# Layer B attention: scores three steps ahead instead of two from step 11 on, with a fourth buffer for the softmax weights

## The chip, the cores and the metric

The kernel runs on one core of one Trainium2 chip. Such a core has five engines that run side by side, each through its own list of instructions, in that list's order: TensorE (PE in the profile), which multiplies matrices and also transposes them; VectorE (DVE); ScalarE (ACT); GpSimd (POOL); and SyncE (SP), which here only starts transfers. An engine waits when its next instruction needs something that another engine has not yet delivered; nothing behind that instruction can overtake it.

TensorE writes its results to PSUM, and everything else (operands, weights, softmax weights) lies in SBUF. PSUM is used here as eight banks of 128 partitions by 512 numbers: the kernel takes six of them for matrix products (tag `mm`) and two for transposes (tag `tr`).

The metric is the device time of one execution in microseconds (us), the median over the runs of a kernel; lower is better.

## The reference

The program is a two-layer decoder trunk on 512 tokens of width 1024, all in 32-bit floating point. Layer A is a latent attention with eight heads over all earlier tokens, layer B is a sliding-window attention. After each comes an MLP with a squared ReLU. The part that matters here is the attention of layer B, for 16 query heads of 64 dimensions that share 4 key and value heads:

```python
s = einsum('bnqkgd,bnjkd->bnkgqj', q, k_band) * SWA_HEAD_DIM ** -0.5   # blocks of 128 queries, bands of 256 keys
s = where(mask, s + bias, -inf)          # relative-position bias, window of 128, causal
m = maximum(s.max(-1), sink)
p = exp(s - m[..., None])
denom = p.sum(-1) + exp(sink - m)
p = p / denom[..., None]
o = einsum('bnkgqj,bnjkd->bnqkgd', p, v_band)
y = o.reshape(B, S, 1024) @ w_o
x = layernorm(alpha * x + y)
```

## The kernel before

**Precision.** Each operand is kept as a rounded high part and a low part that holds the rest. A product is the sum of three products of parts (`three`), and a `split` is one ScalarE copy (the high part) and one subtraction on VectorE or GpSimd (the low part). In the score products of layer B the query holds both parts stacked along its 128 rows, so that two matmuls suffice.

**Order of the work.** The kernel is written as one list of calls. A scheduler at compile time fixes every engine's list from it: TensorE's instructions and most transfers are held in the order of the program (`pe(...)` says so), while those of VectorE, ScalarE and GpSimd are taken, when their engine is free in the scheduler's own clock, from those that are ready, those that stand earlier in the program first; what is traced under `high_priority` goes ahead of that. Buffers are given out in the same pass: a tile of a tag gets one of the tag's buffers once it is free, and its first writer waits for the last reader of the tile that was there.

**Layer B's attention** is run by `run_steps` (L552) with one step per head, `u = 0 ... 15`, after two steps that only start things (`ahead = 2`). Step `u` does, in TensorE's order:

1. `scores(u + 2)` (L1331): eight matmuls into two new `mm` banks, four query blocks in all. Then, off TensorE: VectorE adds the bias in place and takes the row maxima (L1354, four times) and makes from them the negative maxima `nb` (L1358); ScalarE takes the four exponentials from the two banks into the SBUF tile `p` with the row sums (L1362) and the sink's term `ri` (L1366); VectorE adds and inverts (L1367, L1368); GpSimd scales `p` by the result (L1369, L1371).
2. the fills that are due at this step: other work of TensorE that is put between the heads. Up to step 10 these are the queries of later heads (`queries`, 12 matmuls a call, two calls for a pair of heads); from step 11 on they are the first parts of the output projection, `proj.part(t, kp)` of L501, six matmuls each, which add the weight chunk `kp` to the projection of the token block `t`. The bank of a token block is taken at its first part and kept until the projection is finished.
3. `turn(u)` (L1374): seven transposes of `p` of head `u` into the two `tr` banks; ScalarE and VectorE split them to `pth` and `ptl` (L77, L81), which frees the `tr` banks.
4. `mix(u - 1)` (L1397): eight matmuls of values and transposed weights into one `mm` bank; ScalarE copies half of it (`low`, L1413), VectorE adds the other half (`o`, L1414), which frees the bank. After every second head ScalarE and GpSimd split `o` to `oh` and `ol` (L77, L81), the operands of the output projection.

The fills around the change are

```python
fill.append((0, 11, 11, preloads[1]))
for t, kp, u in ((0, 0, 11), (0, 1, 12), (1, 0, 13), (1, 1, 13), (2, 0, 14), (2, 1, 14), (0, 2, 15), (1, 2, 15), (2, 2, 16)):
```

that is, token block 0 takes its bank at step 11, block 1 at step 13, block 2 at step 14; `preloads[1]` starts two transfers of the following MLP's weights. The last two queries (heads 14 and 15) are made in one bank by `queries(7, 0)` and `queries(7, 1)`; this bank becomes free when VectorE has made the low part of head 15's query (L1326).

**Buffers.** `p` of layer B has three buffers of 4 KiB a partition, the transposed weights two each, the small tiles `nb`, `sm` and `ri` three each. The pool of layer B's attention lies in SBUF where the pool of the last MLP lies afterwards.

Of the kernel before, what the change touches and what calls it, by code (L numbers as in the profile page):

```python
# [8 lines left out]
F32 = mybir.dt.float32  # L9
# [6 lines left out]
P = 128  # L16
D = 1024
S = 512
NT = S // P
# [6 lines left out]
SQH, SKVH, SHD = 16, 4, 64  # L26
# [15 lines left out]
AHEAD_S, AHEAD_B = 3, 2  # L42
# [6 lines left out]
def build(tc, nc, io, out):  # L49
    with ExitStack() as top:  # L50
        cp = top.enter_context(tc.tile_pool(name="cp", bufs=1))
# [10 lines left out]
        def nm(s):  # L62
            n_names[0] += 1
            return f"{s}_{n_names[0]}"
# [10 lines left out]
        def split(dst_h, dst_l, src, engine=None, keep=False):  # L75

            high = nc.scalar.activation(dst_h, src, AF.Copy)  # L77
            if keep:
                pe(high)
            with behind(state.pop("open", None)):  # L80
                low = (engine or nc.vector).tensor_sub(dst_l, src, f32(dst_h))  # L81
            if pinned[0] and engine is None:
                pe(low)
            return high, low

        def pe(ins):
            tc.keep_in_program_order(ins)
# [15 lines left out]
        def group(dst, pairs, first=True, last=True, **kw):  # L103
            for i, (st, mv) in enumerate(pairs):
                pe(nc.tensor.matmul(  # L105
                    dst, st, mv, start=first and i == 0, stop=last and i == len(pairs) - 1, **kw
                ))
# [252 lines left out]
        nc.gpsimd.memset(f32(zeros), 0.0)  # L360
        b = bank()
        group(b.rearrange("p (a b) -> p a b", a=4), [(zeros, zeros[:, None, :].broadcast_to([P, 4, P]))] * WARM)
        dummy = cp.tile([P, 1], F32, name="dummy")

        x0 = Feat()
        xraw = [xp.tile([P, 4, S], F32, tag="xt", bufs=8, name=nm("xraw")) for _ in range(2)]
# [40 lines left out]

        ident = cp.tile([P, P], F32, name="ident")
        pe(nc.sync.dma_start(ident, io["ident"]))
        gq = cp.tile([P, 3], F32, name="gq")  # L410
        pe(nc.sync.dma_start(gq, io["g_q"]))
        gkv = cp.tile([P, 2], F32, name="gkv")
        pe(nc.sync.dma_start(gkv, io["g_kv"]))
        sink = cp.tile([P, SQH], F32, name="sink")
        pe(nc.sync.dma_start(sink, io["sinks"].partition_broadcast(P)))
# [3 lines left out]
        pe(small)  # L419
        relh, rell = [cp.tile([33, SQH], F32R, name=nm("rel")) for _ in range(2)]  # L420
        split(relh, rell, relb)
        half = cp.tile([P, 1], F32, name="half")
        nc.gpsimd.memset(half, -0.5)
        sink8 = cp.tile([P, SQH], F32, name="sink8")
        nc.vector.tensor_scalar(sink8, sink, 8.0, None, ALU.mult)
# [123 lines left out]
                    for t in range(NT):  # L549
                        self.evac(t, slice(512, D), bs[t])  # L550

        def run_steps(units, ahead, scores, turn, mix, fill, per, lag, rest):  # L552

            total = sum(f[0] for f in fill)
            n, spent, at = len(units), 0.0, 0
            for u in range(-ahead, n):
                if u + ahead < n:
                    scores(*units[u + ahead])  # L560
                target = total * (u + ahead + 1) / (n + ahead)
                while at < len(fill) and (spent < target or fill[at][1] <= u) and fill[at][2] <= u:
                    fill[at][3]()
                    spent += fill[at][0]
                    at += 1
                if u < 0:
                    continue
                turn(*units[u])
                if u >= lag and (u - lag) % per == per - 1:
                    mix(units[u - lag][0])  # L570
            for f in fill[at:]:
                f[3]()
            for f in rest:
                f()
            for u in range(n, n + lag):
                if (u - lag) % per == per - 1:
                    mix(units[u - lag][0])
# [339 lines left out]
        with tc.tile_pool(name="mla", bufs=1) as mp:  # L917
# [222 lines left out]
            def scores(h, i):  # L1140
                a = heads[h]
                kk = a["k"]
                qh, ql = a["q"]
                n = (i + 1) * P
                tq = slice(i * P, n)
                b = bank()
                p = scratch()
                mask = cmask[:, 512 - n :]
                if i == 0:

                    two = b[:, 0:256].rearrange("p (a b) -> p a b", a=2)
                    group(
                        two, [(qh[:, tq], kk[:, :, :n]), (a["qr"][:, tq], krr[:, :, :n])], True, False,
                        skip_group_check=True,
                    )
                    group(b[:, :n], [(ql[:, tq], kk[:, 0, :n])], False, True, skip_group_check=True)
                    nc.vector.tensor_add(p[:, :n], b[:, n : 2 * n], mask)
                    mask = p[:, :n]
                else:
                    group(  # L1160
                        b[:, :n],
                        three(qh[:, tq], ql[:, tq], kk[:, 0, :n], kk[:, 1, :n])
                        + [(a["qr"][:, tq], khh[:, :n]), (a["qr"][:, tq], kll[:, :n])],
                    )
                if i == 0:
                    for name in ("mx", "nb", "sm", "ri"):
                        a[name] = sp.tile([P, NT], F32, tag=name, bufs=3, name=nm(name))
                mx, nb, sm, ri = a["mx"], a["nb"], a["sm"], a["ri"]
                one = slice(i, i + 1)
                nc.vector.tensor_tensor_reduce(  # L1170
                    out=b[:, :n], in0=b[:, :n], in1=mask, op0=ALU.add, op1=ALU.max,
                    scale=1.0, scalar=NEG, accum_out=mx[:, one],
                )
                nc.vector.tensor_scalar(nb[:, one], mx[:, one], -MLA_SCALE, None, ALU.mult)
                nc.scalar.activation(
                    p[:, :n], b[:, :n], AF.Exp, bias=nb[:, one], scale=MLA_SCALE, accum_out=sm[:, one]
                )
                nc.vector.reciprocal(ri[:, one], sm[:, one])
                nc.vector.tensor_scalar(p[:, :n], p[:, :n], ri[:, one], None, ALU.mult)
                a["p", i] = p  # L1180
# [38 lines left out]
            fill = []  # L1219
# [34 lines left out]
        with tc.tile_pool(name="swa", bufs=1) as mp:  # L1254
# [76 lines left out]
            def scores(h, _):  # L1331
                j = h // GRP
                q = qs[h]
                nb = sp.tile([P, NT], F32, tag="nb", bufs=3, name=nm("nb"))
                sm = sp.tile([P, NT], F32, tag="sm", bufs=3, name=nm("sm"))
                ri = sp.tile([P, NT], F32, tag="ri", bufs=3, name=nm("ri"))
                bs = []
                for n2 in range(2):
                    b = bank().rearrange("p (a b) -> p a b", a=2)
                    bs.append(b)  # L1340
                    for a in range(2):
                        n = 2 * n2 + a
                        lo_c = P if n == 0 else 0
                        kc = slice(0, P) if n == 0 else slice((n - 1) * P, (n + 1) * P)
                        tq = slice(n * P, (n + 1) * P)
                        group(b[:, a, lo_c:], [(q[:, tq], khh[j][:, kc]), (q[:, tq], kll[j][:, kc])])

                mx = bs[0][:, 0, 0:NT]
                for n2 in range(2):
                    for a in range(2):  # L1350
                        n = 2 * n2 + a
                        lo_c = P if n == 0 else 0
                        b = bs[n2]
                        nc.vector.tensor_tensor_reduce(  # L1354
                            out=b[:, a, lo_c:], in0=b[:, a, lo_c:], in1=bias[h // 2][:, h % 2, lo_c:], op0=ALU.add,
                            op1=ALU.max, scale=1.0, scalar=NEG, accum_out=mx[:, n : n + 1],
                        )
                nc.vector.tensor_scalar(nb, mx, sink8[:, h : h + 1], -SWA_SCALE, ALU.max, ALU.mult)  # L1358
                p = mp.tile([P, NT, 256], F32, tag="p", bufs=3, name=nm("p"))
                for n in range(NT):  # L1360
                    lo_c = P if n == 0 else 0
                    state["exp"] = nc.scalar.activation(  # L1362
                        p[:, n, lo_c:], bs[n // 2][:, n % 2, lo_c:], AF.Exp, bias=nb[:, n : n + 1],
                        scale=SWA_SCALE, accum_out=sm[:, n : n + 1],
                    )
                nc.scalar.activation(ri, nb, AF.Exp, bias=sink[:, h : h + 1])  # L1366
                nc.vector.tensor_add(sm, sm, ri)  # L1367
                nc.vector.reciprocal(ri, sm)  # L1368
                nc.gpsimd.tensor_mul(p[:, 0, P:], p[:, 0, P:], ri[:, 0:1].broadcast_to([P, P]))  # L1369
                rest = ri[:, 1:].unsqueeze(2).broadcast_to([P, NT - 1, 256])  # L1370
                nc.gpsimd.tensor_mul(p[:, 1:, :], p[:, 1:, :], rest)  # L1371
                ps_of[h] = p
# [46 lines left out]
            fill = []  # L1419
# [13 lines left out]
            for m in range(2):  # L1433
                for part in range(2):
                    queries(m, part)
            run_steps([(h, 0) for h in range(SQH)], AHEAD_B, scores, turn, mix, fill, 1, 1, [])

        gb = lambda: load_gb("mix", 1)
        with tc.tile_pool(name="mlp1", bufs=1) as mp:
# [114 lines left out]
```

## Time and profile before

| | us |
|---|---|
| median of three runs | 994.83 |
| lowest and highest of them | 994.56, 996.27 |
| the profiled execution | 995.48 |
| span of its instructions | 993.7 |
| outside the span | 1.78 |
| TensorE busy in the span | 983.7 |
| ScalarE, VectorE, GpSimd busy in the span | 554.3, 773.5, 220.8 |

The profiled execution is 0.65 us above the median and inside the spread of the runs. The profile gives each instruction a start and a duration. Matmuls overlap: one begins before the one before it has ended, so the space between two starts, not a row's own duration, is what one costs when they follow each other, and an idle time that the profile prints (from a modelled end to the next start) is somewhat shorter than the time that was lost. In the rows below, a time is in us from the start of the span, then comes the duration, engine, source line, operation and "written <- read" by the names of the tiles; `x2` marks two instructions shown as one row; a square bracket at the end gives the idle time before it and what ended it.

### The profile page before, as it was taken

Reading aid. Unit: us, or ns where it says so; the run is one execution under the profiler, and the core shown is the slowest. Engines: PE = TensorE matmul, PEld = TensorE weight load, DVE = VectorE, ACT = ScalarE, POOL = GpSimd, SP = SyncE. Lnnn points to the kernel's source line nnn. Section 1 sums busy time; section 2 is a strip of 40 time slices with the busy share of each in tenths; the row PEclk is TensorE's granted clock in tenths of the full one; section 3 lists DMA queues with packets and bytes.
Section 4 is the critical chain, followed back from the end, with each engine's and each line's share of the span. In section 5 each row is a group of like instructions: output and inputs, shape, how many; then the busy total and the mean of one; then the engine's idle time right before and its main releaser. Section 6 shows DMA issues by size and latency. Waiting matters only on the chain.

```text
span 993.7 us, 15822 instructions
## 1 busy us (share of the span) xinstructions
PE 983.7 (99%) x6103; PEld 887.6 (89%) x6103; DVE 773.5 (78%) x1240; ACT 554.3 (56%) x850; POOL 220.8 (22%) x205
## 2 busy tenths in 40 slices
PE   9999999999999999999999999999999999999997
PEld 9888888998899999998898998889998998999986
DVE  6589858989679779786686778798985986898756
ACT  5557643567447537646146799446763663664620
POOL 1331001121312212210002765412121122023000
PEclk9999999999999999999999999999999999999999
DMA  7421237389789878954132213349798698798422
GB/s 262 145 88 43 86 127 208 106 168 236 134 190 238 163 170 229 226 98 148 64 107 96 86 65 103 121 106 213 201 186 186 172 211 173 164 265 144 115 94 85
DMA packets 60678, 149.55 MB, mean 150 GB/s; under 512 B 5259, under 2 KB 10300, under 8 KB 60604
## 3 DMA queue, kind: packets, MB, share of 16 engines
q0 software_dynamic: 24320, 58.73, 33.0%
q1 hardware_dynamic: 36140, 89.56, 26.8%
q8 instruction: 48, 0.79, 0.3%
q10 hardware_dynamic: 144, 0.26, 0.1%
q14 instruction: 26, 0.21, 0.1%
HBM read 146.41 MB, written 4.22 MB: 152 GB/s over the span
## 4 chain that ended last, share of the span: by engine, by line
PE 91%; DVE 3%; DMA 3%; ACT 1%; issue 1%; POOL 0%; DVEq 0%; ACTq 0%; POOLq 0%
PE mm L105 84%; PE tr L105 4%; DMA wq<-in_up 2%; PE tr L1191 1%; DVE wl L81 1%; PE tr L1382 1%; DVE x L456 1%; DVE x L459 1%; DMA raw<-in_w_v 1%; PE tr L1384 0%; ACT wh L77 0%; ACT p L1362 0%; PE tr L698 0%; POOL wl L81 0%; DVE bn L587 0%
## 5 line engine op out<-in xcount | busy, mean ns | idle before, releaser
L105 PE MATMUL mm<-wh,fac 128*128 128x512 f32 (+1 forms) x944 | 292.7, 386 | 0.0
L77 ACT ACTIVATE wh<-wq 128x1024 fp32r<-128x1024 f32 x164 | 173.6, 1060 | 183.8 <-PE mm L105 129.8
L81 DVE TENSOR_TENSOR wl<-wq,wh 128x1024 fp32r<-128x1024 f32 x164 | 199.6, 1221 | 70.6 <-ACT wh L77 69.8
L105 PE MATMUL mm<-xth,wh 128*128 128x256 f32 (+1 forms) x928 | 243.5, 290 | 0.3 <-DVE a L816 0.3
L105 PE MATMUL mm<-xth,wl 128*128 128x256 f32 (+1 forms) x800 | 233.2, 292 | 0.0
L105 PEld LDWEIGHTS mm<-wh,fac 128*128 128x128 f32 x944 | 176.2, 188 | 35.5 <-DVE fac L81 0.8
L105 PE MATMUL mm<-xtl,wh 128*128 128x256 f32 (+1 forms) x672 | 197.1, 293 | 0.0
L105 PE MATMUL mm<-wl,fac 128*128 128x512 f32 (+1 forms) x472 | 182.3, 386 | 0.0
L105 PEld LDWEIGHTS mm<-xth,wh 128*128 128x128 f32 x928 | 168.6, 192 | 3.6 <-issue 0.4
L105 PEld LDWEIGHTS mm<-xth,wl 128*128 128x128 f32 x800 | 153.2, 192 | 2.6
L77 ACT ACTIVATE wh<-raw 128x1024 fp32r<-128x1024 f32 (+3 forms) x86 | 84.9, 989 | 88.9 <-PE mm L105 55.9
L105 PEld LDWEIGHTS mm<-xtl,wh 128*128 128x128 f32 x672 | 128.7, 192 | 3.0
L203 POOL DMA_DIRECT2D wq<-in_up x64 | 77.5, 1237 | 200.7 <-DVE wl L81 193.5
L105 PEld LDWEIGHTS mm<-wl,fac 128*128 128x128 f32 x472 | 88.8, 188 | 16.6
L81 DVE TENSOR_TENSOR wl<-raw,wh 128x1024 fp32r<-128x1024 f32 (+2 forms) x64 | 74.8, 1176 | 32.3 <-ACT wh L77 32.0
L203 POOL DMA_DIRECT2D wq<-in_down x48 | 42.0, 875 | 189.1 <-DVE wl L81 183.2
L81 POOL TENSOR_TENSOR wl<-raw,wh 128x1024 fp32r<-128x1024 f32 (+2 forms) x22 | 46.8, 2130 | 91.4 <-ACT wh L77 69.0
L429 POOL TENSOR_TENSOR rs<-mv,half 128x1 f32<-128x1 f32 x16 | 8.8, 552 | 215.4 <-DVE mv L450 215.4
L105 PE MATMUL mm<-wh,oh 128*128 128x512 f32 x128 | 50.9, 398 | 0.7 <-ACT p L1362 0.7
L105 PE MATMUL mm<-wh,ol 128*128 128x512 f32 x128 | 50.1, 392 | 0.0
L105 PE MATMUL mm<-wl,oh 128*128 128x512 f32 x128 | 50.1, 391 | 0.1
L597 DVE TENSOR_TENSOR x<-mm,x 128x512 f32<-128x512 f32 (+1 forms) x49 | 32.9, 675 | 15.8 <-PE mm L105 15.7
(222 smaller groups left out, 1821.1 us busy)
## 6 DMA issues: line engine op xcount, KB each, us to landing
wq<-in_up POOLq DMA_DIRECT2D x64, 512.0 KB, 8.3
wq<-in_down POOLq DMA_DIRECT2D x48, 512.0 KB, 6.4
wq<-in_up SPq DMA_DIRECT2D x32, 512.0 KB, 5.9
raw<-in_down SPq DMA_DIRECT2D x28, 512.0 KB, 6.9
wq<-in_down SPq DMA_DIRECT2D x24, 512.0 KB, 5.5
raw<-in_up SPq DMA_DIRECT2D x16, 512.0 KB, 4.1
raw<-in_w_o SPq DMA_DIRECT2D x8, 512.0 KB, 4.6
raw<-in_w_sq SPq DMA_DIRECT2D x8, 512.0 KB, 3.2
```

Of the source, the lines that this page charges most:

```text
L77: high = nc.scalar.activation(dst_h, src, AF.Copy)
L81: low = (engine or nc.vector).tensor_sub(dst_l, src, f32(dst_h))
L105: pe(nc.tensor.matmul(dst, st, mv, start=first and i == 0, stop=last and i == len(pairs) - 1, **kw))
L203: nc.gpsimd.dma_start(half(a, jp), chunk(*more, jp), accum_op=ALU.add)
L429: state["rs"] = nc.gpsimd.tensor_tensor(r, v, half, ALU.pow)
L456: pin(nc.vector.scalar_tensor_tensor(x, x, mv[:, 0:1], gb[0], ALU.subtract, ALU.mult))
L459: state["norm"] = nc.vector.scalar_tensor_tensor(x[:, c], x[:, c], r, gb[1][:, c], ALU.mult, ALU.add)
L597: nc.vector.tensor_add(xs[t][:, c], b, xs[t][:, c])
L1191: pe(nc.tensor.transpose(pt[:, kb * P : (kb + 1) * P], p[:, kb * P : (kb + 1) * P], ident))
L1382: pe(nc.tensor.transpose(pt[:, a, 0:P], p[:, kb, P:256], ident))
```

## The change

Three things are changed.

- `run_steps` gets an argument `wider`. From step `wider` on, scores are issued up to three steps ahead instead of two. Layer B passes 11, layer A passes nothing. So at step 11 the scores of heads 13 and 14 are issued one after the other, ahead of that step's fills; at step 12 those of head 15; at step 13 none. Nothing moves before step 11, and no matmul is added or removed.
- `p` of layer B gets four buffers instead of three.
- Four small tiles of the permanent pool (`dummy`, `half`, `gq`, `gkv`) become slices of one tile `few`. Each took a slot of its own; together they give back 96 bytes a partition. The fourth buffer takes 4 KiB of SBUF a partition.

```diff
+        few = cp.tile([P, 8], F32, name="few")
+        dummy, half, gq, gkv = few[:, 0:1], few[:, 1:2], few[:, 2:5], few[:, 5:7]
-        dummy = cp.tile([P, 1], F32, name="dummy")
...
-        gq = cp.tile([P, 3], F32, name="gq")
-        gkv = cp.tile([P, 2], F32, name="gkv")
...
-        half = cp.tile([P, 1], F32, name="half")
...
-        def run_steps(units, ahead, scores, turn, mix, fill, per, lag, rest):
+        def run_steps(units, ahead, scores, turn, mix, fill, per, lag, rest, wider=None):
...
+            begun = 0
             for u in range(-ahead, n):
-                if u + ahead < n:
-                    scores(*units[u + ahead])
+                more = wider is not None and u >= wider
+                while begun < min(u + ahead + 1 + more, n):
+                    scores(*units[begun])
+                    begun += 1
...
-                p = mp.tile([P, NT, 256], F32, tag="p", bufs=3, name=nm("p"))
+                p = mp.tile([P, NT, 256], F32, tag="p", bufs=4, name=nm("p"))
...
-            run_steps([(h, 0) for h in range(SQH)], AHEAD_B, scores, turn, mix, fill, 1, 1, [])
+            run_steps([(h, 0) for h in range(SQH)], AHEAD_B, scores, turn, mix, fill, 1, 1, [], 11)
```

## The prediction

> **What bounds the kernel now.** First the page's busy times, then TensorE's waits in layer B, then the windows of the three steps concerned.
>
> ```profile
> span 993.7 us, 15822 instructions
> PE 983.7 (99%) x6103; PEld 887.6 (89%) x6103; DVE 773.5 (78%) x1240; ACT 554.3 (56%) x850; POOL 220.8 (22%) x205
> ...
> PE mm L105 <- ACT p L1362: 0.7, 1, 0.7
> PE tr L1382 <- DVE ptl L81: 0.3, 1, 0.3
> ...
> 604.80:609.39 4.59, 4.24 (x31) 3.62 (x31) 3.75 (x14) 4.05 (x11) 1.82 (x2) 1.00 0.17 68
> 609.39:613.47 4.08, 4.08 (x31) 3.77 (x31) 3.87 (x15) 3.79 (x13) 1.29 (x1) 1.00 0.02 6
> 613.47:618.20 4.73, 4.03 (x22) 3.25 (x22) 4.02 (x17) 4.65 (x16) 3.06 (x3) 1.00 0.00 0
> ```
>
> TensorE is busy for 99% of the span, and in layer B only two of its waits belong to the stretch that changes: one of 0.7 us for the exponentials (L1362), one of 0.3 us for the split of transposed weights. The window rows (length, then PE, PEld, DVE, ACT, POOL, then clock 1.00) show that around them VectorE and ScalarE are nearly full too: 3.87 of 4.08 us and 4.65 of 4.73 us. So the most that an earlier start of scores can win is about those two waits, and two full engines stand behind what it asks for.
>
> Now TensorE's own list through these steps (first rows of each piece; the row at 614.34 is the last score matmul).
>
> ```profile
> 604.80 0.27 PE L105 MATMUL mm<-skh,q 128*128 128x128 f32 x1
> ...
> 605.79 0.40 PE L105 MATMUL mm<-wh,oh 128*128 128x512 f32 x1
> ...
> 606.95 0.39 PE L105 MATMUL mm<-wh,ol 128*128 128x512 f32 x1
> 607.68 0.30 PE L1382 MATMUL tr<-ident,p 128*128 128x128 f32 x1 [0.35 <-DVE ptl L81]
> ...
> 608.42 0.36 PE L105 MATMUL mm<-pth,vv 128*128 128x256 f32 x1
> ...
> 609.39 0.27 PE L105 MATMUL mm<-skh,q 128*128 128x128 f32 x1
> ...
> 610.43 0.40 PE L105 MATMUL mm<-wh,oh 128*128 128x512 f32 x1
> ...
> 611.82 0.27 PE L1382 MATMUL tr<-ident,p 128*128 128x128 f32 x1
> ...
> 612.50 0.36 PE L105 MATMUL mm<-pth,vv 128*128 128x256 f32 x1
> ...
> 613.47 0.27 PE L105 MATMUL mm<-skh,q 128*128 128x128 f32 x1
> ...
> 614.34 0.28 PE L105 MATMUL mm<-skl,q 128*128 128x256 f32 x1
> 615.32 0.50 PE L105 MATMUL mm<-wh,oh 128*128 128x512 f32 x1 [0.70 <-ACT p L1362]
> ...
> 618.20 0.27 PE L1382 MATMUL tr<-ident,p 128*128 128x128 f32 x1
> ```
>
> Read in order: scores 13, projection part (0,0), turn 11, mix 10, scores 14, part (0,1), turn 12, mix 11, scores 15, parts (1,0) and (1,1), turn 13. Six projection matmuls start 1.16/5 = 0.23 apart (605.79 to 606.95), so part (0,0) is done feeding at 607.18 and turn 11 begins 0.50 late; the score matmuls end feeding at 614.34 + 0.12 = 614.46 and part (1,0) begins 0.86 late. From 605.79 to 618.20 are 12.41 us: 11.05 of work and 1.36 of waits.
>
> **The change part by part.** *Moved:* scores 14 from 609.39 to 605.79, scores 15 from behind mix 11 to behind mix 10. No matmul is added; scores cost 1.04 (609.39 to 610.43) and 0.99 us wherever they stand. What decides is the banks. At 605.79 I count the six `mm` banks as: heads 12 (two, its exponentials run), 13 (two, just written), the queries of 14 and 15 (one), mix 9 (one). Before, part (0,0) and mix 10 take head 12's two as the exponentials end; scores 14 come later and take those of the queries and mix 9. After, scores 14 take head 12's two, and part (0,0), next on TensorE, finds none free. When does one come free?
>
> ```profile
> 604.54 0.20 ACT L1362 ACTIVATION_READ_ACCUMULATOR p<-mm,nb 128x1 f32 x1
> ...
> 605.44 0.20 ACT L1362 ACTIVATION_READ_ACCUMULATOR p<-mm,nb 128x1 f32 x1
> ...
> 605.72 0.96 ACT L77 ACTIVATE pth<-tr 128x512 fp32r<-128x512 f32 x2
> 606.71 0.59 ACT L1325 ACTIVATE q<-mm 64x512 fp32r<-64x512 f32 x1
> ...
> 610.15 0.62 ACT L77 ACTIVATE oh<-o 128x512 fp32r<-128x512 f32 x1
> 610.80 0.37 ACT L1362 ACTIVATE p<-mm,nb 128x128 f32<-128x128 f32 x1
> ...
> 612.41 0.21 ACT L1362 ACTIVATION_READ_ACCUMULATOR p<-mm,nb 128x1 f32 x1
> 612.70 0.98 ACT L77 ACTIVATE pth<-tr 128x512 fp32r<-128x512 f32 x2
> ...
> 623.36 0.98 ACT L77 ACTIVATE pth<-tr 128x512 fp32r<-128x512 f32 x2 [2.14 <-PE tr L1384]
> ```
> ```profile
> 608.38 0.69 DVE L1326 TENSOR_TENSOR q<-mm,q 64x512 fp32r<-64x512 f32 x1
> 609.11 0.68 DVE L1414 TENSOR_TENSOR o<-mm,low 64x512 f32<-64x512 f32 x1
> 609.82 0.22 DVE L1358 TENSOR_SCALAR nb<-mm,sink 128x4 f32<-128x4 f32 x1
> 609.96 1.14 DVE L81 TENSOR_TENSOR ptl<-tr,pth 128x512 fp32r<-128x512 f32 x2
> ...
> 612.40 0.43 DVE L1354 CUSTOM_DVE_ANT_0 mm<-mm,bias 128x256 f32<-128x256 f32 x1
> ...
> 612.87 0.43 DVE L1354 CUSTOM_DVE_ANT_0 mm<-mm,bias 128x256 f32<-128x256 f32 x1
> ...
> 623.99 1.16 DVE L81 TENSOR_TENSOR ptl<-tr,pth 128x512 fp32r<-128x512 f32 x2 [1.04 <-ACT pth L77]
> ```
>
> Head 12's banks are free at 604.74 and 605.64, so scores 14 do not wait: 605.79 to 606.83. The queries' bank is free when VectorE ends head 15's low part, 608.38 + 0.69 = 609.07; mix 9's at 609.11 + 0.68 = 609.79. I keep VectorE's order up to there, since what scores 14 add stands behind it in the program. The hand-over from VectorE to TensorE I take from the chain of work that ended last, ahead of turn 11:
>
> ```profile
> 607.55 0.14 issue
> ```
>
> **First new stall:** 609.07 + 0.14 = 609.21, less 606.83 = **2.38 us**, before a part that waited for nothing. Bounds: 1.30, if VectorE took the query as soon as ScalarE has it (606.71 + 0.59 = 607.30, + 0.69 + 0.14 = 608.13); 3.1, if mix 9's bank is the one given. Behind the waiting matmul stand turn 11, mix 10 and scores 15, and ScalarE's split of turn 11.
>
> Then part (0,0) 1.39, turn 11 0.74, mix 10 0.97 (by the starts above): scores 15 at 612.31. Their banks are head 13's. ScalarE, with turn 11 not there, makes `oh` at 609.85, and 0.65 later (610.15 to 610.80) head 13's exponentials, 1.90 long (610.80 to 612.70): 610.50 to 612.40. The first bank is free a little before scores 15 want it, the second (612.32) half a microsecond later than the first: no wait. Scores 15 end at 613.30, part (0,1) at 614.69; turn 12 wants the `tr` banks of turn 11.
>
> **Second new stall.** Those are free after ScalarE's and VectorE's split of turn 11, which is ready at 611.3. But head 14's exponentials may now go ahead: VectorE, behind `nb` at 609.82, makes the four biases of head 14 at 0.47 each (612.40 to 612.87), 609.96 to 611.84, and its `nb` by 612.1, ahead of 612.40, when ScalarE comes free. They stand earlier in the program than turn 11, so I let them go first: 612.40 to 614.30. Then the split begins on ScalarE, VectorE follows 0.63 behind (623.36 to 623.99) for 1.16: second `tr` bank free at 616.09, and mix 11, in place of 614.69 + 0.68 = 615.37, starts 0.14 and three transposes (0.24) later, at 616.47: **1.10 us**. Bounds: 0, if the split goes first (VectorE is through at 614.2), and 1.9, the exponentials' length.
>
> **Stalls that go:** 0.50 and 0.86, and 0.1 for the slow restart at 615.32 (615.32 to 618.20 is 2.88 for twelve matmuls at 0.23). Turn 13 then starts at 616.47 + 0.97 + 2.78 = 620.22 against 618.20: **+2.0 us**. From there on VectorE and ScalarE have room:
>
> ```profile
> 622.67:627.13 4.46, 4.46 (x28) 3.91 (x27) 2.12 (x4) 2.21 (x4) 1.14 (x2) 1.00 0.00 0
> ```
>
> and TensorE runs without a break, so the 2.0 us are handed to the end.
>
> *Fourth buffer of `p`:* 0. Head 14's exponentials write at 612.40 at the earliest; the buffer that three would give them is that of head 11, transposed by 611.30. So it removes no wait here. Later tiles of the pool lie 4 KiB higher, which changes which of them the last MLP's tiles have to wait for; bounds 0 and, below and above, some tenths. Nothing moves in a transfer queue: scores issue no transfer, and SyncE keeps its order. *The four small tiles in one:* 0. If their writers were chained, the first reader of `half` (L429) would feel it, and GpSimd waits 33.8 us in eight times there for VectorE anyway:
>
> ```profile
> POOL rs L429 <- DVE v L949: 33.8, 8, 16.3
> ```
>
> **Sum.** 2.38 + 1.10 - 0.50 - 0.86 - 0.10 = 2.0 us. The profiled execution would go from 995.48 to 997.5; it stands 0.65 above the median, so the median goes from 994.83 to 996.8.
>
> [...] The rows say PE 99%, PEld 89%. [...]
>
> **The rivals.**
> - *Only the first stall* (0.33): the scheduler sees turn 11 ready before head 14's `nb`, as its clock may differ by the 0.3 us between 612.1 and 612.40. Turn 13 starts at 615.37 + 0.97 + 2.78 = 619.12, +0.9: 995.7. For it: the narrow margin. Against it: at 605.72 the split of turn 10 came only behind head 12's exponentials, though TensorE had begun turn 10 at
>
> ```profile
> 603.15 0.27 PE L1382 MATMUL tr<-ident,p 128*128 128x128 f32 x1
> ```
>
> - *Faster* (0.10): VectorE takes head 15's query at once, the stall is 1.30, and the second does not come. It turns to a gain when the bank is free before 606.83 + 1.46 - 0.14 = 608.15. 1.30 - 1.46 = -0.2: 994.6; if all waits went, -1.46: 993.4. Against it: VectorE took the query at 608.38, 1.1 us after ScalarE had it.
> - *Worse* (0.14): head 14's four biases go ahead of the query on VectorE, up to 1.9 us more on the first stall: 998.7; or mix 9's bank is given, 3.1 in place of 2.38: 997.5.
> - *It does nothing* (0.05): TensorE comes to the same end with its waits elsewhere, 994.8.
>
> **How the numbers follow.** The forecast, both stalls, has 0.38: 996.8, by itself 996.3 to 997.3. The range of 8 in 10 reaches down to the faster case's 994.4 and up to 998.6. A change of 0.2% (2.0 us) is about what a measurement of this kernel can tell from none. The forecast lies on that bound, so half of it counts as slower, with nearly all of "worse" and a little of the second: 0.40. Faster by over 0.2% needs more than all waits on record here: 0.04. Within: 0.56.
>
> **What would show it.** Behind scores 14 on TensorE a gap near 2.3 us, ended by VectorE (L1326, or L1414); the 0.70 row ended by L1362 gone; turn 12 late by about 1.1, ended by L81, with L1362 eight times in a row on ScalarE. It is wrong if part (0,0) follows scores 14 without a gap (another bank was free), if VectorE's row L1326 moves ahead of the splits, or if later stages show new idle time.

## The result, and the profile after

| | before | after |
|---|---|---|
| median, us (7 runs each, taken together) | 995.52 | 998.15 |
| lowest and highest, us | 994.56, 996.27 | 997.80, 999.37 |
| profiled execution, us | 995.48 | 997.80 |

The changed kernel takes 1.003 times as long, with a 95% interval of 1.002 to 1.004: slower, by 2.6 us between the medians and 2.3 us between the two profiled executions.

The head of the page after, and TensorE's waits between 500 and 680 us (engine and line, what it waited for, us in total, times, longest). The lines of the code have moved by one: L1362 of before is L1363 here, L1326 is L1327, L1382 is L1383.

```profile
span 996.0 us, 15813 instructions
PE 984.6 (99%) x6103; PEld 888.8 (89%) x6103; DVE 772.6 (78%) x1240; ACT 554.6 (56%) x850; POOL 221.7 (22%) x205
```
```profile
PE mm L105 <- DVE q L1327: 2.9, 1, 2.9
```

The two waits of before, 0.7 us for the exponentials and 0.3 us for the split, are gone. One of 2.9 us has come, and it is ended by the query's low part on VectorE. The order of the pieces on TensorE is now scores 13, scores 14, part (0,0), turn 11, mix 10, scores 15, part (0,1), turn 12, mix 11, parts (1,0) and (1,1), turn 13. These are rows of its timeline, the first of a piece in most cases; 605.84 is the last score matmul, and 609.53 and 609.95 belong to part (0,0).

```profile
604.03 0.28 PE L105 MATMUL mm<-skh,q 128*128 128x128 f32 x1
...
605.84 0.28 PE L105 MATMUL mm<-skl,q 128*128 128x256 f32 x1
609.02 0.71 PE L105 MATMUL mm<-wh,oh 128*128 128x512 f32 x1 [2.90 <-DVE q L1327]
609.53 0.63 PE L105 MATMUL mm<-wl,oh 128*128 128x512 f32 x1
609.95 0.63 PE L105 MATMUL mm<-wh,ol 128*128 128x512 f32 x1
...
611.66 0.41 PE L1383 MATMUL tr<-ident,p 128*128 128x128 f32 x1
...
613.72 0.27 PE L105 MATMUL mm<-skh,q 128*128 128x128 f32 x1
...
616.10 0.27 PE L1383 MATMUL tr<-ident,p 128*128 128x128 f32 x1
...
620.56 0.27 PE L1383 MATMUL tr<-ident,p 128*128 128x128 f32 x1
```

From the first score matmul of head 13 to turn 13 it was 618.20 - 604.80 = 13.40 us; it is 620.56 - 604.03 = 16.53 us, 3.13 more for the same matmuls. From turn 13 to the end of the span nothing has changed: 993.7 - 618.20 = 375.5 us before, 996.0 - 620.56 = 375.4 us after. So the whole loss lies in these steps. (The execution after reached head 13's scores 0.77 us sooner, over code whose order has not changed; over all twelve profiled kernels this start lies anywhere from 603.59 to 604.80.)

The 3.13 us are made of these terms:

- A gap behind scores 14. They end feeding at 605.84 + 0.12 = 605.96 (0.12 is also the space between the starts at 605.72 and 605.84), and part (0,0) starts at 609.02: 3.06 us.
- Slow matmuls behind the gap. From part (0,0) to turn 11 it is 611.66 - 609.02 = 2.64 us, where before it was 1.39; from turn 11 to scores 15 it is 613.72 - 611.66 = 2.06 us, where before, from turn 12 to scores 15, it was 1.65. Together 1.66 us.
- The waits of before that are gone: -0.50, -0.86 and -0.10.
- The two heads' scores take 1.93 us where I had put 2.03: -0.10.

That is 3.16 against 3.13; the 0.03 comes from rounding and from the choice of the turn that the slow one is compared with. The windows of these pieces show where the slow matmuls come from (length; busy time of PE, PEld, DVE, ACT and POOL with counts; granted clock; DMA share; GB/s):

```profile
604.03:605.96 1.93, 1.93 (x18) 1.88 (x17) 1.15 (x8) 1.91 (x8) 0.00 (x0) 1.00 0.38 153
605.96:609.02 3.06, 0.16 (x2) 0.03 (x1) 3.00 (x13) 1.16 (x2) 1.82 (x2) 1.00 0.01 3
609.02:612.75 3.73, 3.73 (x13) 3.05 (x14) 2.03 (x9) 3.10 (x13) 1.28 (x1) 0.54 0.00 0
```

In the second row TensorE is empty and VectorE is busy for 3.00 of 3.06 us; it is what TensorE waits for. Turn 11, which stands behind part (0,0), does not overtake it: GpSimd had scaled its `p` by 600.37 + 1.47 = 601.84, and VectorE had ended its share of turn 10's split at 607.25 + 0.55 = 607.80, but turn 11 starts at 611.66. In the third the granted clock is 0.54, against 1.00 in all three windows of before: projection matmuls start 0.42 us apart (609.53, 609.95) and not 0.23.

VectorE's list tells why the gap is longer than forecast, and ScalarE's what became of the second stall.

```profile
605.68 0.30 DVE L1355 CUSTOM_DVE_ANT_0 mm<-mm,bias 128x128 f32<-128x128 f32 x1
...
606.91 0.42 DVE L1355 CUSTOM_DVE_ANT_0 mm<-mm,bias 128x256 f32<-128x256 f32 x1
...
608.18 0.69 DVE L1327 TENSOR_TENSOR q<-mm,q 64x512 fp32r<-64x512 f32 x1
```
```profile
610.28 0.37 ACT L1363 ACTIVATE p<-mm,nb 128x128 f32<-128x128 f32 x1
...
612.17 0.37 ACT L1363 ACTIVATE p<-mm,nb 128x128 f32<-128x128 f32 x1
...
614.05 1.01 ACT L77 ACTIVATE pth<-tr 128x512 fp32r<-128x512 f32 x2
```

Between the start of scores 13 and the query's low part VectorE now does six of the bias steps, four of head 13 and two of head 14 (605.68 and 606.91); before it did four. The query starts 608.18 - 604.03 = 4.15 us after scores 13, where it was 608.38 - 604.80 = 3.58. On ScalarE the exponentials of head 14 (from 612.17) do follow those of head 13, and turn 11's split begins behind them, at 614.05, as forecast. Yet turn 12 starts without a wait at 616.10: VectorE ends its share of that split at 614.97 + 1.12 = 616.09, and TensorE, slowed, comes no sooner.

### The profile page after: what moved, and what is told of

Read it like the earlier page. It is cut to its first block, busy times and chain, and to the rows that moved or that the text cites. A ratio compares the mean times of both kernels' runs of the same rounds, so it can differ in the third digit from the quotient of the medians.

```text
span 996.0 us, 15813 instructions
## 1 busy us (share of the span) xinstructions
PE 984.6 (99%) x6103; PEld 888.8 (89%) x6103; DVE 772.6 (78%) x1240; ACT 554.6 (56%) x850; POOL 221.7 (22%) x205
## 4 chain that ended last, share of the span: by engine, by line
PE 96%; DVE 2%; DMA 1%; ACT 1%; issue 0%; POOL 0%; DVEq 0%; ACTq 0%; POOLq 0%
PE mm L105 88%; PE tr L105 5%; PE tr L1192 1%; PE tr L699 1%; PE tr L1383 1%; DMA raw<-in_w_v 1%; PE tr L1385 1%; DVE wl L81 0%; DMA raw<-in_w_so 0%; ACT wh L77 0%; POOL wl L81 0%; DVE x L454 0%; DVE x L457 0%; PE tr L960 0%; PE tr L469 0%
## 5 line engine op out<-in xcount | busy, mean ns | idle before, releaser
L427 POOL TENSOR_TENSOR rs<-mv,few 128x1 f32<-128x1 f32 x16 | 11.0, 688 | 213.2 <-DVE mv L448 213.2
```

The lines of the kernel that those rows point to most:

```text
L427: state["rs"] = nc.gpsimd.tensor_tensor(r, v, half, ALU.pow)
```

## The experiments

The theory: the stretch is longer because scores 14, issued early, hold the last two free banks, so that TensorE stands until the queries' bank comes free; behind that, head 14's exponentials make turn 11's split late, hidden under the slow matmuls. The rivals: the fourth buffer or the small tiles do it; scores 15 do it; the slow clock alone does it.

The table gives for each kernel its ratio to the kernel before, run beside it, and, from the profiled execution, the time from the start of scores 13 to the end of the span (before: 993.7 - 604.80 = 388.90). The second can be compared across kernels whose matmuls stand in another order; it comes from one execution each, and the spans are printed to 0.1 us.

| kernel | median, us (runs) | before beside it | ratio (95% interval) | scores 13 to end, less 388.90 |
|---|---|---|---|---|
| the change | 998.15 (7) | 995.52 | 1.0030 (1.0020, 1.0040) | +3.07 |
| three_buffers | 997.82 (6) | 994.85 | 1.0029 (1.0017, 1.0040) | +3.17 |
| memory_only | 994.65 (11) | 994.85 | 0.9999 (0.9990, 1.0007) | -0.01 |
| query_low_first | 999.05 (5) | 994.85 | 1.0038 (1.0026, 1.0051) | +3.56 |
| gap_filled | 998.56 (5) | 994.85 | 1.0035 (1.0021, 1.0048) | +3.27 |
| only_14_early | 998.36 (5) | 995.21 | 1.0035 (1.0023, 1.0048) | +4.05 |
| half_of_14_early | 994.76 (11) | 995.21 | 0.9998 (0.9989, 1.0007) | 0.00 |
| only_15_early | 995.46 (11) | 995.21 | 1.0005 (0.9996, 1.0013) | +0.41 |
| gap_filled_turn_first | 996.59 (11) | 994.81 | 1.0016 (1.0007, 1.0025) | +1.69 |
| parts_earlier | 994.06 (11) | 995.21 | 0.9991 (0.9982, 1.0000) | -0.55 |
| parts_earlier_even | 994.01 (11) | 994.81 | 0.9989 (0.9980, 0.9998) | -0.98 |

**The buffers.** First the change with three buffers of `p`:

```diff
-                p = mp.tile([P, NT, 256], F32, tag="p", bufs=4, name=nm("p"))
+                p = mp.tile([P, NT, 256], F32, tag="p", bufs=3, name=nm("p"))
```

> The changed kernel with three buffers of the softmax weights instead of four; the order on TensorE is that of the changed kernel. Theory (the six matrix banks are all taken behind scores 14, TensorE stands for 3.06 us until VectorE frees the bank of the last queries, and then runs for 3.7 us at half its clock): the fourth buffer is no part of it, so the time stays within 0.5 us of the changed kernel's, about +2.6 us over the kernel before, with the same gap and the same slow stretch. Rival (the fourth buffer, or the places that tiles get in SBUF because of it, costs the time): +0 to +0.5 us over the kernel before.

and then the buffers and the small tiles alone, with the scores where they were:

```diff
-            run_steps([(h, 0) for h in range(SQH)], AHEAD_B, scores, turn, mix, fill, 1, 1, [], 11)
+            run_steps([(h, 0) for h in range(SQH)], AHEAD_B, scores, turn, mix, fill, 1, 1, [])
```

> The kernel before with only the memory edits: four buffers, and the four small tiles in one. The scores stay two steps ahead. Theory (banks): within 0.5 us of the kernel before. Rival (buffer or SBUF places): about +2.6 us.

With three buffers the time is that of the change (1.0029), and so is the gap, to the hundredth:

```profile
608.71 0.47 PE L105 MATMUL mm<-wh,oh 128*128 128x512 f32 x1 [2.90 <-DVE q L1327]
...
609.25 0.40 PE L105 MATMUL mm<-wh,ol 128*128 128x512 f32 x1
609.49 0.58 PE L105 MATMUL mm<-wh,oh 128*128 128x512 f32 x1
609.86 0.63 PE L105 MATMUL mm<-wl,oh 128*128 128x512 f32 x1
```

The memory alone costs nothing that can be measured (0.9999). So the memory edits have no share in the loss that these runs can see, and the fourth buffer has no use here. These rows also show the slow stretch setting in 0.8 us after the gap, in the middle of a part: from 609.25 to 609.49 it is 0.24 us, from 609.49 to 609.86 it is 0.37. The last section comes back to that.

**Which scores.** Only head 14's scores early:

```diff
-                more = wider is not None and u >= wider
+                more = wider is not None and u == wider
```

> The changed kernel with scores 14 early as there, but scores 15 at their old place behind mix 11. Theory (the bank that part (0,0) lacks at step 11 is the whole loss): the same gap of 3.06 us behind scores 14 and the slow clock behind it, so +2 to +3 us over the kernel before. Rival (the third step ahead of scores 15 has a share): clearly less than the changed kernel's loss, +1 or below.

only head 15's early (the last argument of `run_steps` is 12, not 11):

```diff
-            run_steps([(h, 0) for h in range(SQH)], AHEAD_B, scores, turn, mix, fill, 1, 1, [], 11)
+            run_steps([(h, 0) for h in range(SQH)], AHEAD_B, scores, turn, mix, fill, 1, 1, [], 12)
```

> The wider lead begins at step 12: scores 14 at their old place, scores 15 right behind them, ahead of part (0,1). Theory (banks): at that moment the six banks hold part (0,0), mix 10, heads 13 and 14, so scores 15 wait for head 13's exponentials (banks free at 611.5 and 612.3 on the time scale of the kernel before, wanted at 610.43): 1.2 to 2 us of new wait, less about 0.9 that goes (the wait ahead of part (1,0)): 0 to +1.5 us, and up to 1.6 more if the clock falls. Rival (it is only step 11 that is short of banks): a gain of 0.5 to 0.9 us.

and only the first half of head 14's, which takes one bank and not two; its second half and all of head 15's stand where they stood before:

```diff
-                for n2 in range(2):
-                    b = bank().rearrange("p (a b) -> p a b", a=2)
...
+                if h != 14:
+                    opened(h)
+                    products_of(h, 0)
+                products_of(h, 1)
...
+                if h == 13:
+                    opened(14)
+                    products_of(14, 0)
+                    biased(14, 0)
```

> Only the first half of scores 14 (query blocks 0 and 1, one bank) is issued at step 11, the second half at its old place; scores 15 at their old place. One matrix bank is asked for early instead of two. Theory (banks): part (0,0) finds head 12's second bank free and follows without a gap; the wait for the last queries' bank moves to mix 10 and is 0.7 us, too short for the clock to fall; about +0.5 to +1 us over the kernel before, against +2.6 for two banks. Rival (scores ahead cost because VectorE gets their biases ahead of the queries, whatever the banks): a gap near 3 us stays, +2 us or more.

TensorE's rows of the three, in this order: for head 14 alone the end of the scores, part (0,0), the second and the last matmul of part (0,1), and turn 12; for head 15 alone the start of its scores; for the half, the last score matmul, part (0,0) and mix 10. The last row is VectorE's, the query's low part in the half.

```profile
606.26 0.28 PE L105 MATMUL mm<-skl,q 128*128 128x256 f32 x1
609.44 0.47 PE L105 MATMUL mm<-wh,oh 128*128 128x512 f32 x1 [2.90 <-DVE q L1327]
609.98 0.40 PE L105 MATMUL mm<-wh,ol 128*128 128x512 f32 x1
610.21 0.39 PE L105 MATMUL mm<-wh,oh 128*128 128x512 f32 x1
...
613.78 0.40 PE L105 MATMUL mm<-wh,ol 128*128 128x512 f32 x1
616.21 0.30 PE L1383 MATMUL tr<-ident,p 128*128 128x128 f32 x1 [2.03 <-DVE ptl L81]
```
```profile
610.55 0.33 PE L105 MATMUL mm<-skh,q 128*128 128x128 f32 x1 [1.18 <-ACT p L1363]
```
```profile
605.73 0.28 PE L105 MATMUL mm<-skl,q 128*128 128x256 f32 x1
605.85 0.40 PE L105 MATMUL mm<-wh,oh 128*128 128x512 f32 x1
...
609.30 0.38 PE L105 MATMUL mm<-pth,vv 128*128 128x256 f32 x1 [0.46 <-DVE q L1327]
```
```profile
608.55 0.69 DVE L1327 TENSOR_TENSOR q<-mm,q 64x512 fp32r<-64x512 f32 x1
```

Head 14 alone loses as much as the whole change (1.0035; 3.15 us between the medians, just above the 2 to 3 that were expected), with the same gap of 609.44 - 606.38 = 3.06 us. Head 15 alone is within the measurement of before (1.0005): its scores then wait 1.2 us for a bank of head 13's and give back the 0.70 us wait that they save. The half of head 14's scores costs nothing that can be measured (0.9998), where 0.5 to 1 us was expected, and part (0,0) follows them without a gap, 0.12 us after the last of them. So there was one free bank to spare at step 11, and not two. That settles the banks. VectorE is as late as in the change: its query starts 608.55 - 604.40 = 4.15 us after scores 13, to the hundredth as there, behind the same six bias steps. But with one bank fewer asked for, part (0,0) no longer needs the queries' bank; mix 10 takes it, and waits 0.46 us (the mean granted clock of these runs is 0.997 to 0.999, as in the kernel before). So the order of VectorE's work alone does not make the gap.

**What sets the length of the gap.** Here the bias steps of heads 13 and 14 come behind the query's low part on VectorE, so that the queries' bank comes free sooner:

```diff
-                    nc.vector.tensor_sub(q[other, cols], b[own, :], f32(q[own, cols]))
+                    state["q_low"] = nc.vector.tensor_sub(q[other, cols], b[own, :], f32(q[own, cols]))
...
-                        nc.vector.tensor_tensor_reduce(
+                        with behind((state["q_low"],) if h in (13, 14) else None): nc.vector.tensor_tensor_reduce(
```

> The changed kernel, with the biases of heads 13 and 14 on VectorE put behind the low part of head 15's query, so that the bank that part (0,0) waits for comes free earlier. Theory: VectorE takes the query about 607.0 on the changed kernel's time scale, not 608.18, so the gap is 1.8 us, not 3.06, and too short for the clock to fall: 1.3 us less gap and 1.6 us less slow running, of which some tenths go where head 13's exponentials come later: 2 to 2.9 us below the changed kernel, within 0.7 us of the kernel before. Rival (TensorE waits for something else, or the order alone costs): within 0.7 us of the changed kernel.

It is no faster (1.0038). TensorE's rows are part (0,0), the start of scores 15, and the first two matmuls of the next part; then ScalarE's rows of turn 11's split and the first of head 13's exponentials.

```profile
607.30 0.47 PE L105 MATMUL mm<-wh,oh 128*128 128x512 f32 x1 [1.49 <-DVE q L1327]
...
612.34 0.33 PE L105 MATMUL mm<-skh,q 128*128 128x128 f32 x1 [1.77 <-ACT p L1363]
...
613.91 0.63 PE L105 MATMUL mm<-wh,oh 128*128 128x512 f32 x1
614.34 0.63 PE L105 MATMUL mm<-wl,oh 128*128 128x512 f32 x1
```
```profile
609.45 0.98 ACT L77 ACTIVATE pth<-tr 128x512 fp32r<-128x512 f32 x2 [0.36 <-PE tr L1385]
...
611.38 0.37 ACT L1363 ACTIVATE p<-mm,nb 128x128 f32<-128x128 f32 x1
```

The first gap did shrink, from an idle time of 2.90 to 1.49 us, as the forecast of the query's role has it. But the delayed bias steps make head 13's exponentials late (611.38), scores 15 want that head's banks, and TensorE waits 1.77 us there, then runs slow: the granted clock was 1.00 from 607.30 to 610.30, behind the first gap, and 0.56 from 612.34 to 616.20, behind the second. The gain that was expected in time is a miss: the wait moved by one head.

**The slow clock.** To keep TensorE busy through the gap without changing anything else, the four matmuls into head 14's second bank are done five times, which gives the same numbers:

```diff
+                for n in (2, 3) * (4 if h == 14 else 0): group(bs[1][:, n - 2, :], [(q[:, n * P : (n + 1) * P], k[j][:, (n - 1) * P : (n + 1) * P]) for k in (khh, kll)])
```

> The changed kernel, with the four matmuls of head 14's second bank made five times instead of once (16 matmuls more, the same values, 1.9 us of work put into the gap). The wait for the bank is left as it is. Theory with the clock as its second half: the next part starts at the same moment as in the changed kernel, but at full clock, so the six matmuls behind it are 0.23 apart and not 0.42: about 1.6 us below the changed kernel, +1.0 over the kernel before, though it does more work. Rival (the slow matmuls wait for their operands or for a port, not for the clock): the slow stretch stays, within 0.4 us of the changed kernel.

TensorE's rows: scores 13, part (0,0), the last matmul of part (0,1), turn 12, turn 13.

```profile
604.63 0.27 PE L105 MATMUL mm<-skh,q 128*128 128x128 f32 x1
...
609.62 0.47 PE L105 MATMUL mm<-wh,oh 128*128 128x512 f32 x1 [0.98 <-DVE q L1327]
...
610.15 0.40 PE L105 MATMUL mm<-wh,ol 128*128 128x512 f32 x1
610.39 0.39 PE L105 MATMUL mm<-wh,oh 128*128 128x512 f32 x1
...
614.89 0.39 PE L105 MATMUL mm<-wh,ol 128*128 128x512 f32 x1
616.39 0.30 PE L1383 MATMUL tr<-ident,p 128*128 128x128 f32 x1 [1.11 <-DVE ptl L81]
...
621.26 0.30 PE L1383 MATMUL tr<-ident,p 128*128 128x128 f32 x1 [0.20 <-DVE ptl L81]
```

Part (0,0) comes 609.62 - 604.63 = 4.99 us after scores 13, just as in the change (609.02 - 604.03 = 4.99), and now runs at full speed, 0.24 apart. So the slow stretch does go with TensorE's idle time here: with 0.98 us of it in place of 2.90, the granted clock was 1.00 from 609.62 to 613.40, where the change had 0.54 behind its gap. But the time won is not kept: turn 12 waits 616.39 - 614.89 - 0.23 = 1.27 us for turn 11's split, and comes 11.76 us after scores 13, against 616.10 - 604.03 = 12.07 in the change. This is the second stall of the prediction, which the slow matmuls had covered; the time stays where it was (1.0035), and my expectation of a gain missed.

If that is so, then taking the second stall out too must pay. In the next kernel the gap is filled as above, and head 14's exponentials (`finished(14)`) stand behind turn 11's split on ScalarE:

```diff
+                for n in (2, 3) * (4 if h == 14 else 0):
...
+                if h == 11:
+                    with behind(state["turned"][:1]):
+                        finished(14)
```

> The kernel with the filled gap, and head 14's exponentials on ScalarE put behind the split of turn 11 (in the filled kernel they stood ahead of it). Theory (the second new stall of the forecast is real: turn 12 stands behind those exponentials when the clock does not fall): the 1.27 us ahead of turn 12 go, and of the 0.36 ahead of turn 13 little stays; from scores 13 to turn 13 it takes 15.0 to 15.5 us, not 16.63 (kernel before: 13.40), about 1.1 to 1.6 us below the filled kernel. Rival (the wait ahead of turn 12 belongs to something else, such as VectorE's load): 16 us or more stay.

ScalarE's rows (turn 11's split, the first of head 14's exponentials), and TensorE's (scores 13, turn 12, turn 13):

```profile
611.95 0.98 ACT L77 ACTIVATE pth<-tr 128x512 fp32r<-128x512 f32 x2
612.80 0.39 ACT L1379 ACTIVATE p<-mm,nb 128x128 f32<-128x128 f32 x1
```
```profile
603.81 0.27 PE L105 MATMUL mm<-skh,q 128*128 128x128 f32 x1
...
614.30 0.27 PE L1399 MATMUL tr<-ident,p 128*128 128x128 f32 x1
...
618.76 0.27 PE L1399 MATMUL tr<-ident,p 128*128 128x128 f32 x1
```

Turn 12 has no wait, and scores 13 to turn 13 take 618.76 - 603.81 = 14.95 us, just below the 15.0 to 15.5 that were expected. The ratio falls to 1.0016, 2.0 us below `gap_filled`. What is left up to turn 13, 14.95 - 13.40 = 1.55 us, agrees with the first stall alone, less what the change saves: 3.06 - 0.50 - 0.86 - 0.10 - 0.10 = 1.50.

**Is there a better place?** The waits of before can be had in another way: not scores earlier, but projection parts, which need one bank each and no softmax. The kernel before, with only its list of fills changed:

```diff
-            for t, kp, u in ((0, 0, 11), (0, 1, 12), (1, 0, 13), (1, 1, 13), (2, 0, 14), (2, 1, 14), (0, 2, 15), (1, 2, 15), (2, 2, 16)):
+            for t, kp, u in ((0, 0, 11), (0, 1, 11), (1, 0, 12), (1, 1, 12), (2, 0, 13), (2, 1, 13), (0, 2, 14), (1, 2, 14), (2, 2, 15)):
```

> The kernel before, scores two steps ahead, three buffers; the parts of the output projection are put one to a step earlier: (0,0) and (0,1) at step 11, (1,0) and (1,1) at 12, (2,0) and (2,1) at 13, (0,2) and (1,2) at 14, (2,2) at 15. Work that needs no new bank is put where VectorE and ScalarE are late. Theory (steps 11 and 12 are short of matmuls to cover 4.2 us of VectorE's work a step, and (0,1) needs no bank of its own): the wait of 0.5 us ahead of turn 11 goes, that of 0.86 stays or moves to part (1,0) at step 12: 0 to 1 us below the kernel before. Rival (part (1,0) at step 12 meets the bank shortage in full): +0.5 to +2.

and a second form, in which the last two are `(1, 2, 15), (2, 2, 16)`:

> The kernel before with the parts of the projection earlier as in the run with earlier parts, but spread to the last step: (0,0) and (0,1) at step 11, (1,0) and (1,1) at 12, (2,0) and (2,1) at 13, (0,2) at 14, (1,2) at 15, (2,2) behind the steps. Theory: the new wait of 0.22 us ahead of mix 15 in that run goes, the wait of 0.4 ahead of part (1,0) stays: 0.5 to 1.1 us below the kernel before. Rival: turn 14 and 15 now come before their softmax weights are ready, 0 to +0.5.

TensorE's rows of the second: scores 13, turn 11, the last matmul of scores 14, part (1,0).

```profile
604.68 0.27 PE L105 MATMUL mm<-skh,q 128*128 128x128 f32 x1
...
608.42 0.27 PE L1382 MATMUL tr<-ident,p 128*128 128x128 f32 x1
...
610.94 0.28 PE L105 MATMUL mm<-skl,q 128*128 128x256 f32 x1
611.47 0.50 PE L105 MATMUL mm<-wh,oh 128*128 128x512 f32 x1 [0.25 <-ACT p L1362]
```

The 0.50 us ahead of turn 11 is gone, and the 0.86 ahead of part (1,0) has become 611.47 - 611.06 = 0.41. From scores 13 to the end of the span it is 0.98 us less, and the ratio is 0.9989 (0.9980 to 0.9998): about 0.1% faster than the kernel before. The first form is level with it (0.9991). That is half of the 0.2% named in the prediction, but the interval, from 11 runs of one and 21 of the other, lies just below 1.

## Why the prediction was right or wrong

The time, 998.15 us against a forecast of 996.8, lies in the range. The kernel before ran 0.69 us higher in the runs taken beside it than in the three known at the time; against its own companion the change cost 2.6 us where 2.0 was forecast.

*Six banks, all taken at step 11:* right, and shown by three kernels: one bank fewer asked for, and no gap; head 14 alone, the same gap; three buffers, the same gap. The bank that ended the wait was the queries', by L1327, and the hand-over from VectorE's end (608.87) to TensorE's start (609.02) was 0.15 against the 0.14 taken from the chain of waits.

*First stall 2.38 us:* it measured 3.06, at the upper bound of 3.1. The step that failed is "I keep VectorE's order up to there, since what scores 14 add stands behind it in the program". Program order decides only between steps that are both ready, in the scheduler's clock; two bias steps of head 14 were ready before the query was and went ahead of it, 0.57 us (4.15 - 3.58), and the other 0.10 is the scores that ended sooner than forecast. (That clock is not on record. In the trace ScalarE had the query's high part ready at 606.53, and the second of the two steps, at 606.91, still went ahead; so it was the order fixed at compile time, and not readiness on the chip, that put it there.) This is half of the rival called "worse", which put four bias steps there.

*Second stall 1.10 us:* its cause was right and its effect was not seen. ScalarE did take head 14's exponentials ahead of the split, and not by the 0.3 us that were forecast: their `nb` was there at 610.57 + 0.22 = 610.79, 1.38 us before ScalarE came free at 612.17. But TensorE, later and slower than forecast, came to turn 12 when the banks were free. With the gap filled the stall is there, 1.27 us; with the gap left and the clock at full speed (1.00 from 609.44 to 616.21 in `only_14_early`) it is 616.21 - 613.78 - 0.23 = 2.20 us, though there no scores 15 stand in front of it; and with the order turned round it goes. The time that I gave to it was spent elsewhere.

*The granted clock:* no term of the sum. It took 1.66 us in the profiled execution. Net it cost little: without it the second stall takes nearly the same time, 16.63 us (621.26 - 604.63, in `gap_filled`) against 16.53 from scores 13 to turn 13.

*Waits that go, 0.50, 0.86 and 0.10:* right, and all three were gone. *Scores 15 without a wait:* right in the change, where head 13's exponentials are done before 612.17 and scores 15 begin at 613.72. They do wait where they come sooner against those exponentials, 1.77 us in `query_low_first` and 1.18 in `only_15_early`. *Fourth buffer and small tiles 0:* right. *Later work unchanged:* right, 375.5 against 375.4 us from turn 13 on.

So the sum of the terms was 0.7 us too small for the first stall and 0.6 too small in what followed it (1.66 of slow matmuls in place of 1.10 of stall), less 0.1 for the scores counted already in the first. That the total came so near is in part luck: a term that the sum lacked, the slow clock, stood where the second stall was put, and covered it. The rival "only the first stall" (995.7) described a kernel that could be made, `gap_filled_turn_first` at 996.6, but not this one.

## What to carry to other kernels

Before work is issued further ahead, count what it holds: here a step that stood in no one's way when it asked for one PSUM bank (0.9998) cost 0.3% when it asked for two, and a fourth buffer in SBUF could not help, since it was not what ran out. Where a short wait on TensorE is to be filled, take the work that needs the fewest results of the full engines: projection parts won 0.1% where scores, each with a softmax behind them, lost 0.3%. And when one wait is taken away, look for the next late engine behind it before counting the gain: three of these kernels took away a stall or a slow stretch, and got about the same time back from the next one.

## What the runs showed of the hardware

I had not expected the clock. After a gap of 3.06 us (2.90 by the profile's idle time) TensorE was granted half its clock, 0.50, for 3.41 us, from 609.08 to 612.50 in the change; in the gap, and again from 612.50 on, it was 1.00. In `three_buffers`, after the same gap, the first three matmuls ran at full speed (the next starts come 0.31, 0.23 and 0.24 later, where `gap_filled` at full clock has 0.30, 0.23 and 0.24), and the slow stretch began at 609.5 and lasted about as long: projection matmuls start 0.43 apart in it (609.86 and 610.29), and the spacing is that of before again from 613.0 on. In the profiled execution of `only_14_early` there was none in this part: the granted clock was 1.00 from 606.30 to 616.21, over a gap of 3.06 and a second of 2.20 us (2.90 and 2.03 of idle time), and the transposes behind the second gap are 0.11 apart, as in the kernel before. In `query_low_first` it did not come behind the first gap (1.49 us of idle time), but behind the second, of 1.9 us (1.77 of idle time). So the length of one gap does not decide: 1.77 us of idle time stood ahead of a slow stretch in one execution, and 2.90 us ahead of none in another. What does decide is not shown by these runs.

The mean granted clock of the other runs agrees as far as it can. The traces of the kernel before and of the change also have half the clock at the end of the span (0.50 from 991.4 us on, where TensorE has no more work), and the runs of the kernel before have means of 0.997 to 0.999, so 0.997 alone tells nothing. But 0.995 and 0.996 stand only in runs of kernels with a long gap: in six of the seven of the change, all six of `three_buffers`, and three of the five each of `only_14_early` and `query_low_first`. All five of `gap_filled` have 0.998.
